# A hybrid gMLP and dilated-attention trunk on one core: side work moved between the quarters, v scaled on POOL, output combinations loaded an item ahead

## The chip, the core and the metric

The kernel runs on one core of one Trainium2 chip. The metric is the time of one execution on the device in microseconds. Three runs of the kernel before gave 2929.86, 2934.66 and 2934.5 us, median 2934.5. The engines are named as the profile names them: PE (TensorE matmul), PEld (its weight loads), DVE (VectorE), ACT (ScalarE), POOL (GpSimd), SP (SyncE, which issues the DMAs).

## The reference

The input x has 2048 rows of 1024, c is one conditioning vector. Layer A is a gated MLP whose gate mixes rows within chunks of 128; layer B is dilated sliding-window attention with 24 heads in three groups (distances 1, 4, 16), all reading one shared K/V. Everything is float32.

```
# layer A
shift, scale, gate = split(silu(c) @ ada_w + ada_b, 3)
h = rms_norm(x, norm_g) * (1 + scale) + shift
u, v, z = split(h @ w_in, 3)                   # each 2048 wide
u = gelu(u);  v = rms_norm(gelu(v), sgu_g)
mixed = einsum('gts,bcsge->bctge', tril(w_s), v per chunk) + b_s
x = x + gate * ((u * mixed * silu(z)) @ w_out)
# shared k, v from the new x: 6 heads each, k normalised
# layer B
q, z = h' @ w_in_b                             # 24 query heads, gate z
per group: softmax over the previous and own band of 128 keys, ALiBi bias, log-sum-exp
o = sum over groups of softmax(lse) * o_group
x = x + gate * ((o * silu(z)) @ w_out_b)
```

## The kernel before

The 2048 rows are worked in four quarters of 512 (Q = 0 to 3). A matrix product in float32 is done by splitting each operand into a high and a low part of the form that TensorE multiplies fast; three matmuls stand for one. Operand and weight are split by an ACT copy (L262) and a DVE subtraction (L263), 128 x 512 at a time. Large products are also done in Strassen's way: seven products of combined blocks stand for eight, with combined weights (t1 to t4) that are made once, kept in DRAM (wt, cw, wtd) and loaded again.

The order of the stages in the program is: layer A of quarter 0 (its v, u, z and its output product, L1325), layer B of quarter 0 (proj_B, L1539: blocks kv2, kv1, q2, kv0, q1, q0, z); then layer_half (L1402), which makes v, u and z of layer A for quarters 1 and 2 together: first the column blocks vh4 and vh5 of v, then eight gate blocks, each of a u part (uh0 to uh7) and a z part (zh0 to zh7); then output product and layer B of quarter 1, the same of quarter 2, layer A of quarter 3 (v3, u3, z3, output product), layer B of quarter 3, and the last attention with the final product.

Beside the products runs side work. It is written as generators in a list called fillers (L76); at certain matmuls tick (L92) adds the current rate[0] to a counter and lets the generators at the front of the list make as many steps as the counter has whole units. drain (L98) runs the list out. So a rate sets how densely a piece of side work lies beside the products, and the place in the program where it is appended sets where it begins. A scheduler then orders the instructions of each engine, and buffers come from pools with a fixed number of tiles.

The pieces of side work that the change touches are these. combine_out (L431) makes the combined output weights: for each of 8 items it loads two 512 KB tiles co (L441), subtracts among the four parts (L460), splits the results into cs and stores them with DMAs wtd<-cs (L457); an item has six steps, three of them empty ones between its loads and its first subtraction. presplit_b (L417) loads the sixteen blocks of the last output weights (pre, L411), splits them and stores the parts (wod, L407). ada_gate and ada_acc (L180, L233) make a conditioning vector on DVE from eight 512 KB loads. make_h(1) (L865) makes the second part of the normalised long input for quarters 1 and 2, with a load xa, PE transposes (pt_a, L896) and DVE scalings (h_a, L898). attend_local and near (L1836, L1839) are attention over blocks of 128 queries; there POOL makes dg (L1772), a select (L1773), an addition (L1775) and adds into pT (L1799), which PE reads (po, L1824). In the gate blocks each tile vc of v is loaded (L1440) and scaled by the rows' factor rvh on ACT (L1444) before PE mixes it (pmh, L1452). All DMAs named here are issued by SP in one order.

Of the kernel before, what the change touches and what calls it, by code (L numbers as in the profile page):

```python
# [1 line left out]

# [32 lines left out]
def trunk(ctx, tc, out, x, c, a_ada_w, a_ada_b, a_norm_g, a_w_in, a_sgu_g, a_w_spatial,  # L35
# [144 lines left out]
    def ada_acc(res, w, c0, nm):  # L180

        acc = evt(f"acc_{nm}")
        for k in range(KT):
            if k % 2 == 0:
                wt = xp.tile([P, 2, 512], F32, tag="xin", name=f"aw_{nm}{k}")
                nc.sync.dma_start(wt, w[k * P:(k + 2) * P, c0:c0 + 512].rearrange("(k p) n -> p k n", p=P))
# [46 lines left out]
    def ada_gate(w, b, i, nm):  # L233
        for h in range(2):
            res = []
            cs = slice(h * 512, (h + 1) * 512)
            yield from ada_acc(res, w, 2 * D + h * 512, f"{nm}{h}")
# [179 lines left out]
    def presplit_b():  # L417

        t = one.tile([P, 8, 512], F32R, tag="big", name="pre")
        todo = [(b_w_out[k * P:(k + 1) * P, n * 512:(n + 1) * 512], wod[n, k]) for n in range(2) for k in range(KT)]  # L420
        return presplit(todo, lambda i, u: t[:, 4 + 2 * (i % 2):6 + 2 * (i % 2), :] if u else
                        t[:, i % 4, :].bitcast(F32))

    def presplit_a():

        todo = [(a_w_out[(8 * h + 4 * r + k) * P:(8 * h + 4 * r + k + 1) * P, c * 512:(c + 1) * 512], wtd[h, 4 + r + c, k])
                for h in range(2) for r, c in ((0, 0), (1, 0), (1, 1)) for k in range(4)]
        return presplit(todo, lambda i, u: wp.tile([P, 2, 512], F32R, tag="w", name=f"was{i}") if u else
                        rp.tile([P, 512], F32, tag="raw", name=f"rawa{i}"))
# [3 lines left out]
    def combine_out():  # L433


        for h in range(2):
            for k in range(4):
                q = []
                for r in range(2):
                    t = cb.tile([P, 2, 512], F32, tag="xin", name=f"co{h}{k}{r}")  # L440
                    nc.sync.dma_start(t, a_w_out[(8 * h + 4 * r + k) * P:(8 * h + 4 * r + k + 1) * P, :]  # L441
                                      .rearrange("p (c n) -> p c n", c=2))
                    q += [t[:, c, :] for c in range(2)]
                yield
                yield
                yield
                t1, t3, t4, t2 = q
# [799 lines left out]
    def layer_A(Q, hA, m, sqv, j0):  # L1247
        if Q:
# [3 lines left out]
            rate[0] = 3.9  # L1252
# [139 lines left out]
    def in_long():  # L1392
        p = presplit_a()
        for n, _ in enumerate(attend_local(0, True)):
            if n % 4 == 3:
                next(p, None)
            if n == 50:
                rate[0] = 1.1
# [3 lines left out]
    def layer_half(ops, got):  # L1402
# [26 lines left out]
        for g in range(8):  # L1429
            if g == 2:  # L1430
# [5 lines left out]
                rate[0] = 1.7  # L1436
            vch = []
            for half in range(2):
# [100 lines left out]
    def proj_B(Q, hk, hb, keep, rest, ahead, ready):  # L1539
# [72 lines left out]
        if Q == 1:  # L1612
            rate[0] = 2.4
# [505 lines left out]
```

## Time and profile before

| what | us |
|---|---|
| runs | 2929.86, 2934.66, 2934.5; median 2934.5 |
| profiled execution | 2929.71 |
| its span, first to last instruction | 2928.0 |
| PE busy | 2858.4 (98%) |
| DVE busy | 2196.6 (75%) |
| ACT busy | 1655.4 (57%) |
| POOL busy | 756.7 (26%) |
| mean granted TensorE clock | 0.995 |

The profile is of one execution, and its times are microseconds from the start of the span. A row of a window gives the busy time of each engine in that stretch with the number of its instructions, then the granted clock of TensorE (1.00 is 2.4 GHz, 0.50 is 1.2 GHz), the mean busy share of the DMA engines, and the data rate. A row of a wait names the waiting instruction's line and the instruction or DMA that released it. In a timeline the bracket at a row's end is the idle time before it and what ended it. The stages lie, roughly, at 0 to 412 (layer A of quarter 0), 412 to 632 (layer B of quarter 0), 640 to 809 (vh4 and vh5), 810 to 1222 (gate blocks), 1222 to 1530 (quarter 1), 1530 to 1855 (quarter 2), 1855 to 2640 (quarter 3), and the rest.

### The profile page before, as it was taken

How to read it: one execution, taken by the hardware profiler on the slowest of the kernel's cores; microseconds unless marked ns; L12 is line 12 of the kernel's file. 1: busy time of each engine (PE TensorE's matmuls, PEld its weight loads, DVE VectorE, ACT ScalarE, POOL GpSimd, SP SyncE). 2: the span in 40 equal slices, each digit the busy share in tenths (PEclk: the TensorE clock that was granted, in tenths of full speed). 3: DMA queues.
4: the chain of work that ended last, by engine and by line, in shares of the span. 5: the costliest groups of instructions: out<-in, count | busy, mean ns of one | idle time of the engine just before them, and what ended most of it. 6: DMA issues, size and time to landing. Idle time of an engine off the chain costs nothing.

```text
span 2928.0 us, 45185 instructions
## 1 busy us (share of the span) xinstructions
PE 2858.4 (98%) x14450; PEld 2390.7 (82%) x14450; DVE 2196.6 (75%) x4104; ACT 1655.4 (57%) x3390; POOL 756.7 (26%) x1021
## 2 busy tenths in 40 slices
PE   8999999999999999999999999999999999999999
PEld 5788878877888787777888888888888888888887
DVE  6877468687597788867787867789779776888782
ACT  4324436666566676536564557667655366876441
POOL 1066332340000013001424224205335221222312
PEclk9999999999999999999999999999999999999999
DMA  9899786788776644687999858864337967789653
GB/s 320 288 333 342 260 287 201 231 285 287 274 266 191 212 152 165 232 316 258 315 325 329 281 175 264 292 195 138 116 110 255 334 202 227 254 269 335 221 173 110
DMA packets 388209, 718.74 MB, mean 245 GB/s; under 512 B 42010, under 2 KB 121084, under 8 KB 387588
## 3 DMA queue, kind: packets, MB, share of 16 engines
q1 hardware_dynamic: 387972, 715.87, 72.9%
q8 instruction: 114, 1.87, 0.3%
q14 instruction: 123, 1.01, 0.1%
HBM read 541.52 MB, written 174.20 MB: 244 GB/s over the span
## 4 chain that ended last, share of the span: by engine, by line
PE 71%; DVE 9%; DMA 8%; ACT 5%; issue 4%; POOL 2%; SPq 1%; POOLq 0%; DVEq 0%; ACTq 0%
PE pd_kv L291 8%; PE po L1824 3%; PE pd_o L291 2%; PE pd_u L333 2%; PE pd_u L335 2%; PE pd_u L334 2%; PE pd_z L333 2%; PE pd_z L335 2%; PE pd_z L334 2%; PE pd_v L291 2%; PE pd_o3a L291 2%; PE pq L1714 1%; PE pd_o1a L291 1%; PE pd_o2a L291 1%; PE ps L1745 1%
## 5 line engine op out<-in xcount | busy, mean ns | idle before, releaser
L291 PE MATMUL pd_kv<-w_kv,hkh 128*128 128x512 f32 x672 | 208.9, 391 | 2.3 <-DVE w_kv L263 2.0
L1824 PEld LDWEIGHTS po<-kv,pT 128*128 128x128 f32 x1200 | 149.8, 193 | 23.5 <-POOL pT L1799 9.1
L1824 PE MATMUL po<-kv,pT 128*128 128x128 f32 x1200 | 154.5, 278 | 12.8 <-POOL pT L1799 7.0
L291 PEld LDWEIGHTS pd_kv<-w_kv,hkh 128*128 128x128 f32 x672 | 125.6, 188 | 30.0 <-DVE w_kv L263 2.9
L1772 POOL TENSOR_TENSOR dg<-pr,ident 128x256 f32<-128x256 f32 x38 | 32.5, 855 | 429.6 <-ACT pr L1764 405.1
L291 PE MATMUL pd_kv<-w_kv,hkl 128*128 128x512 f32 x336 | 130.7, 389 | 0.0
L1764 ACT ACTIVATE pr<-pr,stat,rt 128x256 f32<-128x256 f32 (+1 forms) x192 | 104.2, 544 | 28.9 <-DVE stat L1761 14.2
L262 ACT ACTIVATE w_q<-raw_q 128x512 fp32r<-128x512 f32 x144 | 88.9, 627 | 54.1 <-DMA raw_q<-in_b_w_in_dram 12.2
L1588 POOL TENSOR_SCALAR s_q<-s_q 128x4 f32<-128x4 f32 x96 | 29.0, 302 | 346.6 <-DVE s_q L1587 260.7
L263 DVE TENSOR_TENSOR w_q<-raw_q,w_q 128x512 fp32r<-128x512 f32 x144 | 96.7, 693 | 26.2 <-ACT w_q L262 24.2
L2012 PE MATMUL pf<-wo,yb 128*128 128x512 f32 x256 | 104.8, 409 | 0.2 <-ACT yb L1975 0.2
L333 PE MATMUL pd_u<-hAh,w_u 128*128 128x512 f32 x256 | 103.6, 405 | 0.0
L333 PE MATMUL pd_z<-hAh,w_z 128*128 128x512 f32 x256 | 102.6, 401 | 0.0
L2014 PE MATMUL pf<-wo,yb 128*128 128x512 f32 x256 | 100.4, 392 | 0.0
L335 PE MATMUL pd_u<-hAh,w_u 128*128 128x512 f32 x256 | 100.2, 391 | 0.0
L2013 PE MATMUL pf<-wo,yb 128*128 128x512 f32 x256 | 100.2, 391 | 0.0
L335 PE MATMUL pd_z<-hAh,w_z 128*128 128x512 f32 x256 | 100.1, 391 | 0.0
L334 PE MATMUL pd_z<-hAl,w_z 128*128 128x512 f32 x256 | 99.9, 390 | 0.0
L334 PE MATMUL pd_u<-hAl,w_u 128*128 128x512 f32 x256 | 99.9, 390 | 0.0
L1764 ACT ACTIVATE st_pr<-st_pr,stat,rt 128x256 f32<-128x256 f32 (+1 forms) x128 | 73.4, 575 | 25.4 <-DVE stat L1758 14.7
L262 ACT ACTIVATE w_u<-raw_u 128x512 fp32r<-128x512 f32 x64 | 40.0, 628 | 81.4 <-PE pd_u L335 52.6
L1799 POOL TENSOR_TENSOR pT<-pT,dg 128x256 f32<-128x256 f32 x76 | 62.8, 831 | 89.1 <-DVE pT L1798 78.3
(1474 smaller groups left out, 8960.0 us busy)
## 6 DMA issues: line engine op xcount, KB each, us to landing
raw_q<-in_b_w_in_dram SPq DMA_DIRECT2D x144, 256.0 KB, 3.9
qt<-qd SPq DMA_DIRECT2D x96, 260.0 KB, 3.4
od<-ot SPq DMA_DIRECT2D x96, 256.0 KB, 3.0
w_o<-wtd SPq DMA_DIRECT2D x48, 512.0 KB, 5.6
raw_kv<-in_w_kv_dram SPq DMA_DIRECT2D x84, 256.0 KB, 3.6
kv<-kvd SPq DMA_DIRECT2D x75, 256.0 KB, 4.2
raw_u<-in_a_w_in_dram SPq DMA_DIRECT2D x64, 256.0 KB, 3.6
wt<-st_cw SPq DMA_DIRECT2D x64, 256.0 KB, 5.5
```

The costliest lines, as they stand in the source:

```text
L262: nc.scalar.activation(hi, src, AF.Copy)
L263: nc.vector.tensor_tensor(lo, src, hi.bitcast(F32), ALU.subtract)
L291: last_mm[0] = nc.tensor.matmul(pt, a, u[:, w, :], start=f, stop=e, skip_group_check=more)
L333: nc.tensor.matmul(pts[i], wh, hh[:, k, :], start=k == 0, stop=False)
L334: nc.tensor.matmul(pts[i], wh, hl[:, k, :], start=False, stop=False)
L335: nc.tensor.matmul(pts[i], wl, hh[:, k, :], start=False, stop=k == KT - 1)
L1764: nc.scalar.activation(pr[:, i, :], pr[:, i, :], AF.Exp, bias=mneg[:, i:i + 1], scale=u["rt"][:, h:h + 1], accum_out=lsum[:, i:i + 1])
L1799: nc.gpsimd.tensor_tensor(pT[:, :, 0, :], pT[:, :, 0, :], u["dg"][:, c * hp:(c + 1) * hp, :], ALU.add)
L1824: nc.tensor.matmul(po[:, h * P:(h + 1) * P], u["pT"][h // hp][:, h % hp, j, :], u["kv"][:, j, kh, 1, :], start=j == 0, stop=j == nk - 1)
L2012: nc.tensor.matmul(pt, yb[:, 0, k, :], w_[:, 0, :], start=k == 0, stop=False)
L2013: nc.tensor.matmul(pt, yb[:, 0, k, :], w_[:, 1, :], start=False, stop=False)
L2014: nc.tensor.matmul(pt, yb[:, 1, k, :], w_[:, 0, :], start=False, stop=k == KT - 1)
```

## The change

- ada_acc can be given slots: then the four 512 KB loads of a half go out at once, into a tile of their own (gbw), and the steps follow. ada_gate moves from layer B of quarter 0 to layer B of quarter 1 in this form.
- presplit_b takes its tiles from the common pools (wp, rp) and moves from layer B of quarter 1 to quarter 3, where earlier() makes one of its steps after every sixth of the attention's steps.
- make_h(1) moves from the output product of quarter 0 to layer B of quarter 0.
- combine_out loads item i + 1 when it begins item i, and has no empty steps between (two at its start remain).
- the scaling of vc goes from ACT to POOL.
- attend_local(1) beside the output product of quarter 2 does blocks 4 to 6; block 7 and the exchange of its statistics (joint) go to quarter 3.
- rates: 3.9 to 4.9 after v of quarter 3, 4.0 to 2.9 at the output product of quarter 0, 1.1 to 1.15 and 1.7 to 1.5 in the gate blocks, 3.1 to 2.6 at the output product of quarter 2, 0.7 to 0.5 in layer B of quarter 1; 2.0 for make_h(1), 1.2 for ada_gate.

```diff
@@ ada_acc
-    def ada_acc(res, w, c0, nm):
+    def ada_acc(res, w, c0, nm, slots=None):
...
+        if slots is not None:
+            for k in range(0, KT, 2):
+                load(k)
+            yield
@@ presplit_b
-        return presplit(todo, lambda i, u: t[:, 4 + 2 * (i % 2):6 + 2 * (i % 2), :] if u else
-                        t[:, i % 4, :].bitcast(F32))
+        return presplit(todo, own_tiles("b"))
+
+    def own_tiles(nm):
+        return lambda i, u: (wp.tile([P, 2, 512], F32R, tag="w", name=f"w{nm}s{i}") if u else
+                             rp.tile([P, 512], F32, tag="raw", name=f"raw{nm}{i}"))
@@ combine_out
+        nxt = load(0)
+        yield
+        yield
         for h in range(2):
             for k in range(4):
...
-                yield
-                yield
-                yield
-                t1, t3, t4, t2 = q
+                t1, t3, t4, t2 = nxt
+                if 4 * h + k < 7:
+                    nxt = load(4 * h + k + 1)
@@ layer_A
-            rate[0] = 3.9
+            rate[0] = 4.9
...
-            fillers.extend((combine_weights((4, 5), "sums"), make_h(1, affa, None)))
-            rate[0] = 4.0
+            fillers.append(combine_weights((4, 5), "sums"))
+            rate[0] = 2.9
@@ layer_half
-                    nc.scalar.activation(v[:, c, :], v[:, c, :], AF.Copy, scale=rvh[:, i:i + 1])
+                    nc.gpsimd.tensor_scalar(v[:, c, :], v[:, c, :], rvh[:, i:i + 1], None, ALU.mult)
@@ proj_B
-        if Q == 1:
-            rate[0] = 2.4
-            fillers.append(presplit_b())
...
         if Q == 0:
+            rate[0] = 2.0
+            fillers.append(make_h(1, affa, None))
+        if Q == 1:
             rate[0] = 1.2
-            fillers.append(delayed(ada_gate(b_ada_w[0], b_ada_b, 1, "gb")))
-        if Q == 1:
-            rate[0] = 0.8
+            slots = one.tile([P, 4, 2, 512], F32, tag="big", name="gbw")
+            fillers.append(delayed(ada_gate(b_ada_w[0], b_ada_b, 1, "gb", slots)))
@@ attend_local
-        bs = range(4 * Q, 4 * Q + 4)
+        bs = range(4 * Q, 4 * Q + (4 if both else 3))
@@ earlier
-        yield from near(1, True)
-        yield from attend_local(2, True)
+        p = presplit_b()
+        for n, _ in enumerate(chain(attend([(1, 7)], True, 0, 2, True), joint(1), near(1, True), attend_local(2, True))):
+            if n % 6 == 5:
+                next(p, None)
+            yield
+        yield from p
@@ main loop
-                rate[0] = 3.1
+                rate[0] = 2.6
...
-                rate[0] = 0.7
+                rate[0] = 0.5
```

How the scheduled order changes is shown at three places. The first is SP's queue at the end of the output product of quarter 0: x1d<-xr is the store that VectorE waits for, wt<-st_cw are stores of combined weights, raw_kv loads of the next weights, xa the load of make_h(1). Before:

```order
384 L381 DMA wt_0_130<-st_cw_3579 128x512
385 L381 DMA wt_1_131<-st_cw_3584 128x512
386 L381 DMA wt_2_132<-st_cw_3580 128x512
387 L381 DMA wt_3_133<-st_cw_3583 128x512
388 L270 DMA raw_kv_0_0_3774<-in_w_kv_dram 128x512
389 L270 DMA raw_kv_0_1_3779<-in_w_kv_dram 128x512
390 L270 DMA raw_kv_0_2_3784<-in_w_kv_dram 128x512
391 L270 DMA raw_kv_0_3_3789<-in_w_kv_dram 128x512
392 L270 DMA raw_kv_0_4_3794<-in_w_kv_dram 128x512
393 L270 DMA raw_kv_0_5_3799<-in_w_kv_dram 128x512
394 L871 DMA xa_4861<-in_x_dram 128x1024
395 L1344 DMA x1d<-xr_0_2853 128x1024
```

And after, at the same place:

```order
376 L391 DMA wt_2_132<-st_cw_3378 128x512
377 L280 DMA raw_o_1_7_3473<-in_a_w_out_dram 128x512
378 L391 DMA wt_3_133<-st_cw_3381 128x512
379 L280 DMA raw_kv_0_0_3672<-in_w_kv_dram 128x512
380 L280 DMA raw_kv_0_1_3677<-in_w_kv_dram 128x512
381 L280 DMA raw_kv_0_2_3682<-in_w_kv_dram 128x512
382 L280 DMA raw_kv_0_3_3687<-in_w_kv_dram 128x512
383 L280 DMA raw_kv_0_4_3692<-in_w_kv_dram 128x512
384 L280 DMA raw_kv_0_5_3697<-in_w_kv_dram 128x512
385 L1360 DMA x1d<-xr_0_2853 128x1024
```

The load xa is gone from the row ahead of the store, and the last stores wt stand among weight loads where a block of eight stood.

The second place is SP's queue in vh5, ahead of the weights of its last product (raw_vh5t from wt_3; those from wt_2 belong to the product before it). Before:

```order
705 L270 DMA raw_vh5t_1_7285<-wt_2_132 128x512
706 L270 DMA raw_vh5t_2_7290<-wt_2_132 128x512
707 L270 DMA raw_vh5t_3_7295<-wt_2_132 128x512
708 L270 DMA raw_vh5t_0_7374<-wt_3_133 128x512
709 L441 DMA co_7538<-in_a_w_out_dram 128x1024
710 L270 DMA raw_vh5t_1_7379<-wt_3_133 128x512
711 L457 DMA wtd<-cs_7225 128x1024
712 L457 DMA wtd<-cs_7228 128x1024
713 L457 DMA wtd<-cs_7259 128x1024
714 L457 DMA wtd<-cs_7262 128x1024
715 L270 DMA raw_vh5t_2_7384<-wt_3_133 128x512
716 L270 DMA raw_vh5t_3_7389<-wt_3_133 128x512
```

And after, the twelve rows up to the first load of wt_3 (the last load of wt_2 is row 708, and rows 709 to 712 are four stores wtd<-cs):

```order
713 L451 DMA co_7275<-in_a_w_out_dram 128x1024
714 L1406 DMA vh<-vh5b_7245 128x512
715 L1406 DMA vh<-vh5b_7249 128x512
716 L1406 DMA vh<-vh5b_7287 128x512
717 L1406 DMA vh<-vh5b_7291 128x512
718 L473 DMA wtd<-cs_7331 128x1024
719 L473 DMA wtd<-cs_7334 128x1024
720 L473 DMA wtd<-cs_7365 128x1024
721 L473 DMA wtd<-cs_7368 128x1024
722 L451 DMA co_7391<-in_a_w_out_dram 128x1024
723 L451 DMA co_7393<-in_a_w_out_dram 128x1024
724 L280 DMA raw_vh5t_0_7408<-wt_3_133 128x512
```

Fifteen other DMAs stand now between the loads of the two products, where the loads followed each other.

The third is POOL in the last gate blocks, where the near attention runs beside them: dg, select and addition of one head pair, then pT. Before there is nothing between them:

```order
284 L1799 TENSOR_TENSOR pT_1_10_10289<-pT_1_10_10289,dg_1_1_9988 128x2x128
285 L1799 TENSOR_TENSOR pT_1_11_10293<-pT_1_11_10293,dg_1_1_9988 128x2x128
286 L1772 TENSOR_TENSOR dg_2_1_10331<-st_pr_2_10_10317,ident 128x256
287 L1773 AFFINE_SELECT st_pr_2_10_10317<-st_pr_2_10_10317 128x2x128
288 L1775 TENSOR_TENSOR st_pr_2_10_10317<-st_pr_2_10_10317 128x2x128
```

And after:

```order
288 L1813 TENSOR_TENSOR pT_1_00_10145<-pT_1_00_10145,dg_1_0_9858 128x2x128
289 L1813 TENSOR_TENSOR pT_1_01_10149<-pT_1_01_10149,dg_1_0_9858 128x2x128
290 L1460 TENSOR_SCALAR vc_10258<-vc_10258,rvh 128x256 x4
291 L1460 TENSOR_SCALAR vc_10264<-vc_10264,rvh 128x256 x4
292 L1786 TENSOR_TENSOR dg_2_0_10187<-pr_2_00_10173,ident 128x256
293 L1787 AFFINE_SELECT pr_2_00_10173<-pr_2_00_10173 128x2x128
294 L1789 TENSOR_TENSOR pr_2_00_10173<-pr_2_00_10173 128x2x128
```

The eight scalings of a gate block stand between pT of one head pair and dg of the next.

## Rows read from the trace of the kernel before

**Rows 1.** The page, part 1: busy time of each engine, share, instructions.
```profile
PE 2858.4 (98%) x14450; PEld 2390.7 (82%) x14450; DVE 2196.6 (75%) x4104; ACT 1655.4 (57%) x3390; POOL 756.7 (26%) x1021
```

**Rows 2.** Waits of PE: waiting line, releaser, us in total, times, longest.
```profile
PE po L1824 <- POOL pT L1799: 7.0, 5, 3.9
PE pt_a L896 <- DVE h_a L898: 5.4, 5, 2.3
...
PE po L1824 <- ACT pT L1670: 4.7, 3, 2.5
...
PE pt_b L962 <- DVE xr L1354: 3.6, 1, 3.6
...
PE pd_uh6y L743 <- ACT w_uh6t L262: 2.2, 1, 2.2
...
PE pd_q11a L291 <- ACT w_q L262: 1.4, 1, 1.4
```

**Rows 3.** Windows: us, busy PE PEld DVE ACT POOL (count), PEclk, DMA share, GB/s.
```profile
410.00:415.00 5.00, 1.39 (x7) 0.91 (x6) 1.32 (x3) 0.95 (x2) 0.13 (x1) 0.81 1.02 405
415.00:420.00 5.00, 5.00 (x22) 4.41 (x20) 2.82 (x7) 0.49 (x1) 0.00 (x0) 0.51 0.80 253
```

**Rows 4.** Chain of waits, end of quarter 0: start, length, what.
```profile
406.27 7.29 DMA x1d<-xr
```

**Rows 5.** Timeline of SP, end of quarter 0.
```profile
394.79 8.01 SPq L381 DMA_DIRECT2D wt<-st_cw  x8
```

**Rows 6.** The store line L1344, all stores.
```profile
DMA to landing us min/median/max: 2.8/4.1/5.4
```

**Rows 7.** Window of make_h(0) in layer B of quarter 0.
```profile
600.00:650.00 50.00, 47.16 (x219) 37.47 (x218) 44.43 (x67) 30.60 (x53) 23.64 (x31) 1.00 0.85 280
```

**Rows 8.** Timeline of ACT, layer B of quarter 1.
```profile
1354.13 0.63 ACT L262 ACTIVATE pre<-pre 128x512 fp32r<-128x512 f32 x1 [3.83 <-DMA pre<-in_b_w_out_dram]
...
1355.52 0.37 ACT L1522 ACTIVATE hs_k<-pd_kv 128x256 f32<-128x256 f32 x1
```

**Rows 9.** Windows: layer B of quarters 1 and 2, gate blocks.
```profile
1355.00:1360.00 5.00, 2.31 (x8) 1.59 (x7) 3.46 (x7) 3.10 (x7) 2.21 (x4) 0.86 0.43 160
1360.00:1365.00 5.00, 4.44 (x11) 3.00 (x10) 1.72 (x3) 1.88 (x4) 0.30 (x1) 0.50 0.70 185
1698.00:1736.00 38.00, 38.00 (x169) 31.48 (x168) 28.15 (x47) 23.99 (x42) 12.22 (x25) 1.00 0.68 204
955.00:960.00 5.00, 3.92 (x16) 3.48 (x17) 2.88 (x6) 5.00 (x12) 0.00 (x0) 0.66 0.34 106
```

**Rows 10.** Groups by line: busy us, mean ns, idle before, releasers.
```profile
L263 DVE TENSOR_TENSOR w_q<-raw_q,w_q 128x512 fp32r<-128x512 f32 x144 | 96.7, 693 | 26.2 <-ACT w_q L262 24.2 <-DMA qd<-st_q31w 0.9
...
L263 DVE TENSOR_TENSOR w_z<-raw_z,w_z 128x512 fp32r<-128x512 f32 x64 | 58.0, 919 | 31.2 <-ACT w_z L262 29.8 <-DMA st_cw<-in_b_w_in_dram 1.2
...
L1772 POOL TENSOR_TENSOR dg<-st_pr,ident 128x256 f32<-128x256 f32 x38 | 33.5, 880 | 76.8 <-ACT st_pr L1764 67.0 <-DVE stat L1758 2.9 <-DVE stat L1784 2.4
...
L1444 ACT ACTIVATE vc<-vc,rvh 128x256 f32<-128x256 f32 x64 | 27.1, 497 | 15.9 <-DMA vc<-vh 12.7 <-POOL rvh L1427 3.2
...
L1773 POOL TENSOR_SCALAR_AFFINE_SELECT st_pr<-st_pr 128x256 f32<-128x256 f32 x38 | 19.1, 503 | 2.8
```

**Rows 11.** Timeline of ACT in the gate blocks.
```profile
953.06 2.49 ACT L1444 ACTIVATE vc<-vc,rvh 128x256 f32<-128x256 f32 x6
...
1109.75 2.49 ACT L1444 ACTIVATE vc<-vc,rvh 128x256 f32<-128x256 f32 x6
```

**Rows 12.** Windows: a stretch with full queues, and product vh5.
```profile
200.00:250.00 50.00, 50.00 (x247) 42.29 (x246) 31.35 (x33) 16.89 (x27) 33.72 (x25) 1.00 1.02 346
733.00:809.00 76.00, 76.00 (x337) 62.91 (x336) 44.27 (x70) 43.35 (x89) 0.00 (x0) 1.00 0.81 279
```

**Rows 13.** Tile raw_vh5t, its loads.
```profile
DMA to landing us min/median/max: 2.8/3.3/3.8
```

**Rows 14.** Window in the u product of quarter 3.
```profile
1983.70:2003.40 19.70, 19.70 (x127) 17.44 (x126) 19.66 (x52) 12.82 (x30) 13.00 (x16) 1.00 0.43 133
```

More of the change, by code (lines that the diff above doesn't have):

```diff
@@ L1 @@
 from contextlib import ExitStack
+from itertools import chain
 import numpy as np
@@ L177, in trunk, with load @@
                             channel_multiplier=-1)
-    def ada_acc(res, w, c0, nm):
+    def ada_acc(res, w, c0, nm, slots=None):
         acc = evt(f"acc_{nm}")
+        def load(k):
+            wt = xp.tile([P, 2, 512], F32, tag="xin", name=f"aw_{nm}{k}") if slots is None else slots[:, k // 2]
+            nc.sync.dma_start(wt, w[k * P:(k + 2) * P, c0:c0 + 512].rearrange("(k p) n -> p k n", p=P))
+            return wt
+        if slots is not None:
+            for k in range(0, KT, 2):
+                load(k)
+            yield
         for k in range(KT):
             if k % 2 == 0:
-                wt = xp.tile([P, 2, 512], F32, tag="xin", name=f"aw_{nm}{k}")
-                nc.sync.dma_start(wt, w[k * P:(k + 2) * P, c0:c0 + 512].rearrange("(k p) n -> p k n", p=P))
+                wt = load(k) if slots is None else slots[:, k // 2]
             if k == 0:
@@ L231, in ada_affine, with ada_gate @@
         later.append([2, lambda: nc.vector.scalar_tensor_tensor(dst[0], dst[0], 1.0, go, ALU.add, ALU.mult)])
-    def ada_gate(w, b, i, nm):
+    def ada_gate(w, b, i, nm, slots=None):
         for h in range(2):
@@ L427, in presplit_a, with load @@
                 for h in range(2) for r, c in ((0, 0), (1, 0), (1, 1)) for k in range(4)]
-        return presplit(todo, lambda i, u: wp.tile([P, 2, 512], F32R, tag="w", name=f"was{i}") if u else
-                        rp.tile([P, 512], F32, tag="raw", name=f"rawa{i}"))
+        return presplit(todo, own_tiles("a"))
     made = [False]
     def combine_out():
+        def load(i):
+            h, k = divmod(i, 4)
+            q = []
+            for r in range(2):
+                t = cb.tile([P, 2, 512], F32, tag="xin", name=f"co{h}{k}{r}")
+                nc.sync.dma_start(t, a_w_out[(8 * h + 4 * r + k) * P:(8 * h + 4 * r + k + 1) * P, :]
+                                  .rearrange("p (c n) -> p c n", c=2))
+                q += [t[:, c, :] for c in range(2)]
+            return q
+        nxt = load(0)
+        yield
+        yield
         for h in range(2):
             for k in range(4):
[L438 to L443, printed above, removed]
-                yield
-                yield
-                yield
-                t1, t3, t4, t2 = q
+                t1, t3, t4, t2 = nxt
+                if 4 * h + k < 7:
+                    nxt = load(4 * h + k + 1)
                 def keep(*todo):
@@ L1397, in in_long @@
             if n == 50:
-                rate[0] = 1.1
+                rate[0] = 1.15
             yield
@@ L1435, in layer_half @@
                 fillers.append(in_long())
-                rate[0] = 1.7
+                rate[0] = 1.5
             vch = []
@@ L1632, in proj_B @@
         if Q < NQ - 1:
[L1633 to L1634 removed]
+            drain()
             ahead()
@@ L1839, in attend_local, with joint @@
     def attend_local(Q, wrap=False, alt=False, both=True):
-        bs = range(4 * Q, 4 * Q + 4)
+        bs = range(4 * Q, 4 * Q + (4 if both else 3))
         yield from attend([(1, b) for b in bs], wrap, int(alt), 1 + (wrap or alt), wrap or alt)
+        if both:
+            yield from joint(Q)
+            yield from near(Q, wrap, alt)
+    def joint(Q):
         v = stat[1][:, 4 * Q:4 * Q + 4, :]
@@ L1846, in attend_local @@
         nc.sync.dma_start(v, std[1].rearrange("(b i) c -> i b c", i=P)[:, 4 * Q:4 * Q + 4])
-        if both:
-            yield from near(Q, wrap, alt)
     outs = []
```

5 lines of the change are left out of this document (1 added, 4 removed).

## Prediction

> **What bounds the kernel now.** I read the busy line of the page first, then what PE waited for, then short windows round the longest of these waits, and there the timeline of the engine named. PE is busy for 98% of the span [rows 1], and both versions give it the same 13,342 matmuls, so the change can act only on what PE loses: 2928.0 - 2858.4 = 69.6 us of idle time, and the stretches in which its clock is granted at half. The idle time lies in many small places; the longest stand in [rows 2]. A stall can cost twice: at the end of quarter 0 PE does 1.39 us of work in five microseconds, and then works five microseconds at a granted clock of 0.51 [rows 3]. The full-speed work in those ten is 1.39 + 5.00 x 0.51 = 3.9 us, so the place costs 6.1 and not the 3.6 that the waits name. I size every term in this way: idle time, and behind it the busy time at half clock.
>
> **End of quarter 0: -5.5.** PE's first normalisation transposes of layer B (pt_b) wait for VectorE's xr, and that waits for the stores x1d<-xr: 7.29 us from the first one's issue until VectorE can go on [rows 4]. Ahead of it SP has issued eight stores of combined weights in 8 us [rows 5] and, right before it, the load xa of make_h(1); the DMA share is 1.02 while the store is out [rows 3]. In the changed order no load for make_h stands there: six raw_kv loads and then the store, and of the eight stores of combined weights four lie further ahead and four are spread among weight loads. The 16 stores of the line land in 2.8 to 5.4 us, 4.1 in the middle [rows 6]; with 4.1 for the 7.29 the stall of 3.6 shrinks to 0.4. What could remain is the whole term if the kv loads alone fill the queues: -6.1 with 0 as its other end; I take -5.5.
>
> **make_h(1) moved from the output product to layer B of quarter 0: -2.3, +2.** PE waits 2.3 us for h_a once [rows 2], in the product that make_h(1) leaves. It comes back in q02/kv00, where the conditioning (16 accumulations on VectorE) leaves. The nearest row for the same work inside layer B is make_h(0) in the stretch 600 to 650, with 2.84 us idle [rows 7]. I take +2 (0 to +5).
>
> **Layer B of quarter 1: -7.** The weight presplit leaves. There ScalarE sits 3.83 us until a presplit load has landed, and the evacuation hs_k of the PSUM tile that the next product needs stands behind it [rows 8]. The ten microseconds from 1355 hold 2.31 x 0.86 + 4.44 x 0.50 = 4.2 us of full-speed work [rows 9], so 5.8 are lost; a second place of the same kind costs the 1.4 of pd_q11a [rows 2]. Together -7.2. At the same product of quarter 2, without presplit, PE never stops: 38.00 of 38.00 [rows 9]. What comes in instead is ada_gate: eight 512 KB loads, in two groups of four issued at once, and sixteen 128x512 VectorE operations; its 11 us of VectorE (16 x 0.69, the mean of w_q in [rows 10]) I cost at nothing, hidden by VectorE's idle time, which is 9.85 of 38 us at this place of quarter 2 [rows 9]; if that cover is gone, I would give PE at most 3 of the 11. I take -7 (-8 to -3).
>
> **Gate blocks: -6.** The scaling of v goes from ScalarE to POOL: 64 instructions of 497 ns [rows 10]. Two PE stalls hang on them. At 953.06 six scalings (2.49 us) stand ahead of the pT copy for which PE waits 2.5 [rows 2, 11], followed by a clock of 0.66 on 3.92 busy microseconds (1.3 lost) [rows 9]. At 1109.75 another six push the exponentials and three table loads back until w_uh6t comes 2.2 late [rows 2, 11], with about 0.7 at half clock. 2.5 + 1.3 + 2.2 + 0.7 = 6.7. On POOL one 128x256 instruction takes between 0.50 (a select) and 0.88 us (two inputs) [rows 10]; a scaling has one input and no predicate, so I take 0.55. In six of the eight blocks POOL has nothing else to do. In the last two its queue holds the scalings in front of dg and pT of the near attention, where PE already waits for POOL 3.9 us once [rows 2]: eight scalings of 0.55 are 4.4 us in that queue, of which 0 to 4 reach PE; I take +1. The first block's eight scalings end about 1 us later (8 x 0.55 against 3.31), +0.5. Net -5 (-11 to +5).
> VectorE's 128x512 subtraction takes 919 ns on average where POOL combines weights beside it, and 693 in the query weights of layer B [rows 10]. The Trainium skill (GPSIMD Engine Reference, section 1, Specifications) says that POOL shares its SBUF interfaces with VectorE, and that VectorE instructions with two SBUF inputs suffer; the two rows agree. By that rule 64 x 0.55 = 35 us of POOL work would lengthen what VectorE does beside them by up to a third, an estimate of 9 us in the stage; by the rows' bare durations it would be nothing. That is the second rival.
>
> **Output combinations loaded an item ahead: +8.** This is what I fear most. combine_out waits for nothing at each item now, so it takes three turns in place of six, and its transfers fall together in the product of vh5: by the order 4 more loads and 10 more stores, 14 x 0.52 = 7.3 MB, less 1.2 of loads that move on to the gate blocks. The stretch 733 to 809 carries 279 GB/s x 76 us = 21.2 MB [rows 12]; with 6.1 more it asks for 359 GB/s. In fifty microseconds with all queues full the core moved 346 [rows 12]. On SP the four weight loads of the last product (raw_vh5t from wt_3) stood among the loads before; now eight stores wtd<-cs, three co loads and four vh stores stand between the loads from wt_2 and them: 4.2 + 1.6 + 1.0 = 6.8 MB, 20 us at 346 GB/s, and 3 us for the four loads themselves. Between the first use of one product's weights and of the next lie 48 matmuls of 76.00/337 = 0.2255 us [rows 12], 10.8 us, and the wt_2 loads are themselves issued about one product ahead. So 23 us stand against 22, and then come the landing's end (a set's loads land in 3.3 us when nothing is ahead of them [rows 13]), a copy of 0.63 on ScalarE and 0.69 on VectorE: 2 to 5 us too late, and a piece at half clock as at 415 (5.00 x 0.49 = 2.5) [rows 3]: 4.5 to 7.5, and something at the product before, whose lead shrinks as well. I take +8 (0 to +16), since nothing in the trace excludes that SP runs ahead of this order.
> The Trainium skill (DMA: Bandwidth & Descriptors, Where 436 GB/s comes from) gives 358 GB/s as the limit between HBM and one core, and lets it bind. That is 359 against 358, a tie: an estimate of no stall by bandwidth; by the trace's 346 the stage is 3 us short. One stretch of five microseconds shows 405 [rows 3], so the figure is no wall here, and I stay with the 346 of the long stretch.
> What goes is VectorE's wait for the co loads (each lands in about 5 us), but vh5, where most of these waits lie, costs PE nothing before (76.00 of 76.00 busy [rows 12]), and in vh4 the first items stand in the order where they stood, so 0.
>
> **Quarter 2: -2.** Block (1,7) of the attention and its statistics leave layer_out: three blocks for four. Of the 7.0 us that PE waits for POOL's pT, 3.1 lie in four waits under 3.9 [rows 2], most of them there; I take -2 (-4 to 0).
> **Quarter 3: +3.** The block, the presplit (16 loads, 16 ScalarE copies, 16 VectorE subtractions, 16 stores) and a faster rate of side work (4.9 for 3.9) come into u and z. VectorE gets 16 x 0.69 = 11 us and a block's share. It is already full in one stretch, 19.66 of 19.70, where PE still does not stop [rows 14]; the DMA share there is 0.43. So neither stops PE as it is, and what is added lies within about 270 us. Bounds 0 and +8 (most of the 11 us, where they fall on a full VectorE). The other rates that change (1.1 to 1.15, 1.7 to 1.5, 0.7 to 0.5, 3.1 to 2.6, 4.0 to 2.9) place the same side work a little earlier or later among the products; I cost them at nothing, between -2 and +2.
>
> **Sum.** -5.5 - 2.3 + 2 - 7 - 5 + 8 - 2 + 3 = -8.8, about -9 on the profiled execution's 2929.7 (span 2928.0 and 1.7 round it): 2921. The three runs shown are 2929.9, 2934.5 and 2934.7, so the profiled one is at their lower end, and the same -9 from the median gives 2925.5. I take 2922, nearer to the sum since the changed kernel's runs may fall at either end. 0.2% is 5.9 us and about what this kernel's measurement can tell from no change: faster is below 2928.6, slower above 2940.4.
>
> **Rivals.**
> 1. The weights of vh5 starve PE throughout (slower). For it: 359 GB/s asked where 346 were seen; each late set costs 3.3 (landing) [rows 13] + 0.63 [rows 8] + 0.69 = 4.6 us and then about 2.5 at half clock. It decides if SP is held at the stores, so that five sets come late and not one: 5 x 7 = 35 in place of 8, 2949. Three late sets give 21 and 2935. Against it: before, the weights stand well ahead, and stores wait only for copies that VectorE, with 44.27 of 76 busy [rows 12], does early.
> 2. POOL is the wrong place for the scalings (no change): dg and pT come 4 us later in two blocks, VectorE is up to 9 us slower beside POOL, and the -5 turns to +5: 2932. For it: PE already waits 3.9 for POOL, and 919 against 693; against it: POOL is empty in six blocks.
> 3. Quarter 3 can't take the presplit (no change): VectorE full for the added 11 us, +8 and half clock behind it, 2930.
> 4. The change does not do what it says: the kv loads alone make the store late, and the gate's 2 MB at once delay the weights of quarter 1; -5.5 and -7 become -2 and -3: 2930.
>
> **How the numbers follow.** Forecast 0.60 with its own range 2912 to 2930; rival 1 0.16 (two thirds of it slower), rival 2 0.11, rival 3 0.07, rival 4 0.06. Faster: 0.60 x 0.93, and a third of the rest of the mild cases, 0.63. Slower: 0.11 from rival 1, and 0.05 from two of the others together, 0.16. The rest, 0.21, is no change. Range 2907 to 2941: the lower end takes the better ends of vh5 (0) and of the gate blocks, the upper one stops between the two prices of rival 1.
>
> **What would show it.** At the end of quarter 0: x1d under 5 us, and no clock of 0.51 behind it. Layer B of quarter 1: no wait of pd_q12b for hs_k. Gate blocks: no vc on ScalarE, PE's waits for pT of ScalarE and for w_uh6t gone; rival 2 if PE's wait for POOL's pT grows over 7.0. In vh5: PE waiting for w_vh5t or its loads shortly before the first gate block, with a DMA share near 1; without such a wait the +8 is wrong and the time is near 2914. Quarter 3: PE waits in u and z between block 7's operations. If PE's idle time falls by less than 4 us in all, the forecast is wrong.

## The result, and the profile after

The changed kernel takes 2941.8 us (median of 15 runs, 2933.3 to 2949.8) beside 2934.5 for the kernel before (15 runs, 2929.2 to 2942.6): ratio 1.0024, 95% interval 1.0013 to 1.0034. It is a little slower. I had forecast 2922 and a range up to 2941. The profiled executions are 2939.5 (span 2937.8) and 2929.7 (span 2928.0), 9.8 us apart, and the traces account for that.

The first lines of the page after, which answer to [rows 1]: the same 14,450 PE instructions, and idle time of 2937.8 - 2863.8 = 74.0 us, where it was 69.6.

```profile
span 2937.8 us, 45193 instructions
## 1 busy us (share of the span) xinstructions
PE 2863.8 (97%) x14450; PEld 2392.8 (81%) x14450; DVE 2216.8 (75%) x4104; ACT 1639.8 (56%) x3335; POOL 815.2 (28%) x1085
```

What PE waited for, after (waiting line, releaser, us in total, times, longest), against [rows 2]: of the longest waits before, that for xr falls from 3.6 to 0.5. The wait for POOL's pT doubles, in many short pieces where there was one of 3.9, and two new waits of 4.8 and 4.7 stand below it.

```profile
PE po L1838 <- POOL pT L1813: 14.2, 13, 1.7
...
PE pmh L1468 <- POOL vc L1460: 4.8, 1, 4.8
PE pd_vh5a L301 <- ACT w_vh5t L272: 4.7, 1, 4.7
...
PE po L1838 <- ACT pT L1684: 3.6, 4, 1.3
...
PE pt_b L978 <- DVE xr L1370: 0.5, 1, 0.5
```

To place the time by stage I take PE's lost time: from each matmul's start to the next one's, less the median of that distance for matmuls of the same shape before, summed over the stage. It holds idle time, half clock, and the small gaps of a mixed stream. It sums to 117.6 us before and 127.0 after, 9.4 more, nearly the 9.8 by which the executions differ. In quarters 1 to 3 the row of the output product ends at the first q block of layer B, so it holds the two kv blocks before that as well.

| stage | before | after | forecast | measured |
|---|---|---|---|---|
| quarter 0 up to the output product | 26.2 | 24.3 | 0 | -1.9 |
| output product of quarter 0 | 9.8 | 0.1 | -7.8 | -9.7 |
| layer B of quarter 0 | 5.0 | 4.8 | +2 | -0.1 |
| vh4 | 4.4 | 4.2 | 0 | -0.3 |
| vh5 | -0.1 | 8.5 | +8 | +8.6 |
| first gate block, uh0 and zh0 | 0.5 | 7.2 | +0.5 | +6.7 |
| the other gate blocks | 23.9 | 14.9 | -5.5 | -9.0 |
| output product, quarter 1 | 5.7 | 5.6 | 0 | -0.1 |
| layer B of quarter 1 | 7.9 | 0.4 | -7 | -7.5 |
| output product, quarter 2 | 7.4 | 8.2 | -2 | +0.8 |
| layer B of quarter 2 | 0.2 | 0.2 | 0 | 0 |
| v, u, z of quarter 3 | 4.3 | 25.6 | +3 | +21.3 |
| the rest | 22.6 | 23.1 | 0 | +0.5 |

Two windows of after show the places that were mended, the end of quarter 0 (against [rows 3]; start:end, length, busy PE PEld DVE ACT POOL with counts, PEclk, DMA share, GB/s) and the start of q12 in quarter 1 (against the first two of [rows 9]): PE never stops and the clock stays at 1.00. In the first, the store x1d is issued at 396.78 and VectorE's xr follows at 399.84 without a wait.

```profile
395.00:400.00 5.00, 5.00 (x23) 4.13 (x22) 4.05 (x9) 2.79 (x7) 1.46 (x3) 1.00 0.50 195
400.00:405.00 5.00, 5.00 (x31) 4.16 (x30) 4.11 (x8) 1.49 (x3) 0.94 (x1) 1.00 0.72 225
```
```profile
1343.20:1405.60 62.40, 62.40 (x270) 49.50 (x270) 48.67 (x81) 30.12 (x54) 29.21 (x40) 1.00 0.76 242
```

vh5 after (the second row of [rows 12] answers): the queues carry 329 GB/s at a share of 0.93, and after PE's stop the clock is 0.50 for five microseconds. The chain of waits names the load: raw_vh5t, issued at 784.39, takes 5.80 where such loads took 2.8 to 3.8 [rows 13], and the copy and PE follow it. With the 3.3 that was the middle there it would have come 2.5 us earlier; so, as an estimate, half of PE's 4.7 is the load's longer way and the other half its late issue, behind the fifteen other DMAs.

```profile
733.00:790.00 57.00, 52.77 (x232) 43.01 (x230) 38.68 (x63) 31.23 (x66) 0.00 (x0) 1.00 0.93 329
790.00:795.00 5.00, 3.77 (x9) 2.93 (x10) 4.93 (x9) 4.36 (x8) 0.00 (x0) 0.50 1.01 373
```
```profile
784.39 5.80 DMA raw_vh5t<-wt
...
790.55 0.64 ACT w_vh5t L272
...
791.24 1.22 PE pd_vh5a L301 x2
```

The first gate block after. The tile vc (instruction, count, shortest, median and longest in ns): a scaling takes 0.92 us on POOL in the middle, against 0.50 on ACT [rows 10]. In POOL's timeline the eight of the first block end at 818.6, and they start only at 811.29, behind the row factors rvh: on VectorE the sum uh0t stands ahead of these and waits for its load raw_uh, issued at 802.52 and 4.99 us under way.

```profile
L1460 POOL TENSOR_SCALAR vc<-vc,rvh x64: 917/922/1742, 811.3 to 1166.6; 128x256 f32<-128x256 f32 x64
```
```profile
808.46 0.57 POOL L1442 TENSOR_SCALAR rvh<-rvh 128x8 f32<-128x8 f32 x1 [176.13 <-DVE rvh L1441]
809.12 2.07 POOL L1443 TENSOR_TENSOR rvh<-rvh,mhalf 128x8 f32<-128x8 f32 x1
811.29 7.31 POOL L1460 TENSOR_SCALAR vc<-vc,rvh 128x256 f32<-128x256 f32 x8
```

The row factors are late only for a changed order. VectorE has their sums 3.5 us after the block's first matmul (808.21 and 804.71); before it was 5.4 (815.30 and 809.91), and PE did not wait. But the first mixing matmul pmh stood behind 48 of the block's matmuls before and stands behind 12 now. On PE, before and after:

```profile
820.79 1.05 PE L1452 MATMUL pmh<-wst,vc 128*128 128x128 f32 x8
```
```profile
804.71 2.88 PE L759 MATMUL pd_uh0x<-op,w_uh 128*128 128x512 f32 x12
812.35 0.79 PE L1468 MATMUL pmh<-wst,vc 128*128 128x128 f32 x2 [4.76 <-POOL vc L1460]
```

Quarter 3, where most is lost. v, u and z as one window, before and after: PE's idle time goes from 352.10 - 351.04 = 1.1 to 390.70 - 375.06 = 15.6 us, while no engine is full (VectorE 320 of 391, POOL 135). Eleven waits for pT make 12.2 of it (the waits of PE in this stretch); the time at half clock behind them is lost as well.

```profile
1876.20:2228.30 352.10, 351.04 (x1962) 302.03 (x1960) 282.23 (x609) 230.10 (x462) 113.01 (x160) 1.00 0.49 156
```
```profile
1855.30:2246.00 390.70, 375.06 (x2114) 322.41 (x2112) 320.14 (x690) 261.15 (x519) 135.13 (x190) 0.99 0.56 181
```

```profile
PE po L1838 <- POOL pT L1813: 12.2, 11, 1.7
```

One of these waits, on POOL and on PE. PE has transposed pp of one step of the attention at 2163.16, and VectorE's part of pT is done at 2166.4. But the two additions into pT that are left stand in POOL's queue among the work of the next step (dg, a select and an addition, twice over), which waits for that step's exponential (ACT, 2163 to 2165). The last ends at 2171.5, and PE comes to po twice before its half is done.

```profile
2164.52 0.74 POOL L1786 TENSOR_TENSOR dg<-st_pr,ident 128x256 f32<-128x256 f32 x1 [3.38 <-ACT st_pr L1778]
2165.34 0.41 POOL L1787 TENSOR_SCALAR_AFFINE_SELECT st_pr<-st_pr 128x256 f32<-128x256 f32 x1
2165.83 0.74 POOL L1789 TENSOR_TENSOR st_pr<-st_pr 128x256 f32<-128x256 f32 x1
2166.52 1.19 POOL L1786 TENSOR_TENSOR dg<-st_pr,ident 128x256 f32<-128x256 f32 x1
2167.68 1.17 POOL L1813 TENSOR_TENSOR pT<-pT,dg 128x256 f32<-128x256 f32 x1
2168.81 0.86 POOL L1787 TENSOR_SCALAR_AFFINE_SELECT st_pr<-st_pr 128x256 f32<-128x256 f32 x1
2169.75 1.04 POOL L1789 TENSOR_TENSOR st_pr<-st_pr 128x256 f32<-128x256 f32 x1
2170.75 0.72 POOL L1813 TENSOR_TENSOR pT<-pT,dg 128x256 f32<-128x256 f32 x1
```
```profile
2163.16 0.60 PE L1806 MATMUL pp<-ident,pr 128*128 128x128 f32 x4
2168.90 1.16 PE L1838 MATMUL po<-kv,pT 128*128 128x128 f32 x8 [1.02 <-POOL pT L1813]
2171.53 1.63 PE L1838 MATMUL po<-kv,pT 128*128 128x128 f32 x8 [1.47 <-POOL pT L1813]
```

From the last pp transposes to the first po PE took 6.15 us in the middle before (18 cases) and 5.32 after (22 cases), its stops included. From the same transposes to the end of the second addition into pT POOL's queue took 4.8 in the middle before and 5.7 after: what fitted does not fit any more.

### The profile page after: what moved, and what is told of

The parts are those of the page before. It is cut to its first block, busy times and chain, and to the rows that moved or that the text cites. A ratio compares the mean times of both kernels' runs of the same rounds, so it can differ in the third digit from the quotient of the medians.

```text
span 2937.8 us, 45193 instructions
## 1 busy us (share of the span) xinstructions
PE 2863.8 (97%) x14450; PEld 2392.8 (81%) x14450; DVE 2216.8 (75%) x4104; ACT 1639.8 (56%) x3335; POOL 815.2 (28%) x1085
## 4 chain that ended last, share of the span: by engine, by line
PE 73%; DVE 9%; DMA 7%; issue 4%; ACT 3%; POOL 2%; SPq 1%; POOLq 0%; DVEq 0%; ACTq 0%
PE pd_kv L301 7%; PE po L1838 3%; PE pd_o L301 3%; PE pd_v L301 2%; PE pd_z L345 2%; PE pd_z L344 2%; PE pd_z L343 2%; PE pd_o3a L301 1%; PE pd_u L345 1%; PE pd_u L343 1%; PE pd_u L344 1%; PE pd_v3a L301 1%; PE pd_vh4a L301 1%; PE pd_o1a L301 1%; PE pd_v3b L301 1%
## 5 line engine op out<-in xcount | busy, mean ns | idle before, releaser
L1460 POOL TENSOR_SCALAR vc<-vc,rvh 128x256 f32<-128x256 f32 x64 | 61.3, 975 | 190.1 <-DMA vc<-vh 138.2
```

## The experiments

Each undoes a part of the change in the changed kernel. Beside a time stands that of the kernel before on the same chip. All but the last two are single runs, and eleven runs of the kernel before in one series spread from 2920.6 to 2937.3; so a few us between two times say little, and the argument goes by lost times by stage, as above, from one profiled execution each. In runs whose edit leaves a stage alone, vh5 loses 6.0 to 8.5, the first gate block 6.8 to 9.2, uh1 to uh7 12.6 to 15.1, and v, u and z of quarter 3 25 to 30.

**combine_out as before.**

```diff
...
-        nxt = load(0)
-        yield
-        yield
...
-                t1, t3, t4, t2 = nxt
-                if 4 * h + k < 7:
-                    nxt = load(4 * h + k + 1)
+                yield
+                yield
+                yield
+                t1, t3, t4, t2 = q
```

> The changed kernel, with combine_out as before (loads at the head of an item, three empty steps). In the changed kernel PE loses 8.5 us in vh5 (a wait of 4.7 for w_vh5t, and half clock) and 7.2 in the first gate block (a wait of 4.8 for vc). Theory A: both come from the dense transfers; the weights raw_vh5t arrive late, and the load raw_uh that VectorE waits for ahead of the row factors rvh arrives late too. Then vh5 falls to about 0 and the first gate block to 2 or 3: 12 us less, 2929. Rival B: the wait for vc is the price of the scalings on POOL and the place of the first mixing matmul on PE, and has nothing to do with the loads. Then vh5 falls to 0 and the first gate block stays near 7: 8 us less.

2932.5 beside 2928.2. vh5 loses nothing again (-0.1), so the dense transfers were the whole of its 8.5. The first gate block keeps 7.0: for that, rival B seemed right. The first mixing matmul is back behind 48 others, so this edit undoes the order too. PE comes to it later, but the eight scalings took 10.94, and PE still waits 3.1 for vc:

```profile
804.61 10.94 POOL L1455 TENSOR_SCALAR vc<-vc,rvh 128x256 f32<-128x256 f32 x8
```

**Scalings of v on ScalarE.**

```diff
-                    nc.gpsimd.tensor_scalar(v[:, c, :], v[:, c, :], rvh[:, i:i + 1], None, ALU.mult)
+                    nc.scalar.activation(v[:, c, :], v[:, c, :], AF.Copy, scale=rvh[:, i:i + 1])
```

> The changed kernel, with the 64 scalings of v on ScalarE as before. Theory A (late loads hold up rvh): in the first gate block PE still waits, for ScalarE's vc now, some 3 of the 7.2 us; rival B (POOL's price): the first block falls under 1. In the other gate blocks (uh1 to uh7: 23.8 us lost before, 14.9 after) both expect the loss to come back to 20 to 24, with PE's waits for the pT copy of ScalarE and for w_uh6t, so that the whole is within 5 us of the changed kernel.

2936.9 beside 2928.2. The first gate block loses 6.5 all the same: now PE waits 1.4 for w_uh0t and 2.0 for ScalarE's vc, behind the load raw_uh of which VectorE's row tells.

```profile
806.79 0.69 DVE L741 TENSOR_TENSOR uh0t<-raw_uh,uh0t 128x512 f32<-128x512 f32 x1 [1.98 <-DMA raw_uh<-in_w_uz_dram]
807.40 0.16 DVE L1441 TENSOR_REDUCE rvh<-sqh 128x4 f32<-128x16 f32 x1
```

Both theories had missed in part, and what both expected of the other blocks was wrong: they lose 15.7, not 20 to 24. The waits for pT do not come back. That for ScalarE's w_uh6t does, 2.2 before and 1.2 after (with 0.8 more for VectorE's half):

```profile
PE pd_uh6y L759 <- ACT w_uh6t L272: 2.3, 1, 2.3
```

**combine_out as before, and the first block's scalings on ScalarE.**

```diff
...
-                    nc.gpsimd.tensor_scalar(v[:, c, :], v[:, c, :], rvh[:, i:i + 1], None, ALU.mult)
+                    if g == 0:
+                        nc.scalar.activation(v[:, c, :], v[:, c, :], AF.Copy, scale=rvh[:, i:i + 1])
+                    else:
+                        nc.gpsimd.tensor_scalar(v[:, c, :], v[:, c, :], rvh[:, i:i + 1], None, ALU.mult)
```

> The changed kernel with combine_out as before, and with the eight scalings of the first gate block on ScalarE (the other 56 on POOL). Each edit alone left the first gate block at 6.5 to 7 us lost: without the dense loads PE waited for POOL's scalings (three places of 0.4 and one of 3.3), with the scalings on ScalarE it waited for the late row factors. Theory E: the block has two causes, and each covers the other. Then with both undone it falls under 2, and with vh5 at 0 the whole is some 14 us under the changed kernel, 2925. Rival F: the cause is a third one, the place of the mixing matmuls in the order; then it stays above 4.

2929.1 beside 2929.0 (the median of the eleven runs of before in that series). vh5 -0.1, first block 0.1: theory E. The dense transfers and the slow scalings each fill the same gap, and only without both it closes. Rival F is not settled by it: the first mixing matmul is behind 48 others here too, so late loads and changed order went together, and no run parts them.

**Block (1,7) back in quarter 2, rates 3.1 and 3.9.**

```diff
...
-            rate[0] = 4.9
+            rate[0] = 3.9
...
-        bs = range(4 * Q, 4 * Q + (4 if both else 3))
+        bs = range(4 * Q, 4 * Q + 4)
...
-                rate[0] = 2.6
+                rate[0] = 3.1
```

> The changed kernel, with attention block (1,7) back beside the output product of quarter 2, and the rates of before there (3.1) and in quarter 3 (3.9); the presplit stays in quarter 3. From v of quarter 3 to its output product PE loses 4.3 us before and 25.6 after, most of it in eleven waits of 1.2 to 1.9 for POOL's pT. Theory C: the higher rate and the added block put the attention's steps so close together on PE that the chain of exponentials, three POOL instructions and the two pT additions isn't done when PE comes to po. Then the loss falls to 5 to 8: 18 us less. Rival D: the presplit's copies and subtractions stand in that chain on ScalarE and VectorE. Then the loss stays above 15.

2919.3 beside 2928.2. v, u and z of quarter 3 lose 6.1, and 0.9 is left of the waits for pT, with the presplit still among them:

```profile
PE po L1838 <- POOL pT L1813: 0.9, 1, 0.9
```

**The presplit behind the attention.**

```diff
-            if n % 6 == 5:
-                next(p, None)
             yield
         yield from p
```

> The changed kernel, with the presplit's steps behind the attention of quarter 3 and not between its steps; block (1,7) and the rate 4.9 stay. Rival D (the presplit stands in the attention's chain): the loss from v to the output product of quarter 3 falls from 25.6 to under 10, and 15 us are gained. Theory C (rate and block): it stays above 18, and the time changes by less than 6 us.

2964.3 beside 2928.2. u and z still lose 22.0, so the presplit is not the cause; rival D falls. Behind them something new came up: the output product of quarter 3 loses 37.5 (3.4 before), with 17.1 us of waits for its weights w_o3t, which SP issues among the presplit's loads and stores. Behind the attention the presplit costs more than between its steps.

**Rate 3.9 alone.**

```diff
-            rate[0] = 4.9
+            rate[0] = 3.9
```

> The changed kernel with the rate 3.9 of before in u and z of quarter 3; block (1,7) and the presplit stay there. With block and rate both undone the loss from v to the output product of quarter 3 fell from 25.6 to 6.1. Theory C1 (the rate alone sets how close the attention's steps lie): the loss in u and z falls under 8, and what does not fit comes behind, in the output product, where it may cost. Theory C2 (the added block takes its toll by its own instructions): it stays above 15.

2945.3 beside 2929.0. u and z lose 9.2; the block is there, and the waits are gone (1.1 us for pT in all). What does not fit runs behind, and the row of the output product loses 28.6. Theory C1.

**Rate 4.9 alone, the block in quarter 2 with its rate 3.1.**

```diff
-        bs = range(4 * Q, 4 * Q + (4 if both else 3))
+        bs = range(4 * Q, 4 * Q + 4)
...
-                rate[0] = 2.6
+                rate[0] = 3.1
```

> The changed kernel with block (1,7) back beside the output product of quarter 2, but the rate 4.9 kept in u and z of quarter 3. With block and rate undone the loss there was 6.1, with the rate alone undone 9.2, and 28.6 came behind it in the output product. Theory C1 (the rate spaces the steps): with 4.9 the waits for POOL's pT are back, 15 to 25 us. Theory C2 (the block): they are gone, under 9.

2934.2 beside 2932.3. 22.5 lost, without the block, and the waits are back:

```profile
PE po L1838 <- POOL pT L1813: 11.1, 10, 3.3
```

With the run before it this settles quarter 3. The higher rate costs 16.4 with the block (25.6 against 9.2) and 16.4 without it (22.5 against 6.1); the block costs 3.1 at either rate, and at 3.9 it does not fit. In the middle of the cases the way to the second addition into pT takes 5.3 and 5.5 in the two runs at 3.9, where PE takes 6.2 from transposes to po, and 5.8 here, where PE takes 5.7.

**The gate blocks' rates of before.**

```diff
-                rate[0] = 1.15
+                rate[0] = 1.1
...
-                rate[0] = 1.5
+                rate[0] = 1.7
```

> The changed kernel with the gate blocks' rates of before (1.7 and 1.1 for 1.5 and 1.15). The blocks uh1 to uh7 lose 23.8 us before and 14.9 after; with the scalings back on ScalarE they still lose 15.7, so the scalings are not what helped. Theory G: the lower rate is, since the attention's steps lie further apart. Then the loss comes back to 20 or more, about +8 us. Rival H: something else is (the combinations of the output weights are done earlier, and their stores and splits no longer lie in these blocks). Then it stays under 17.

2938.3 beside 2929.0. The blocks uh1 to uh7 lose 15.7: by the sum rival H as against G. But the waits are others. The longest of before is back:

```profile
PE po L1838 <- POOL pT L1813: 3.9, 1, 3.9
```

The three runs with the rates of before (this one, the kernel before and the next) have 3.6 to 3.9 there, and none of the other eleven has it. The eleven, the changed kernel among them, wait 2.2 to 3.5 for w_uh7t, and the three do not; in the changed kernel:

```profile
PE pd_uh7y L759 <- ACT w_uh7t L272: 2.3, 1, 2.3
```

So the rate decides both waits, and they nearly cancel in the sum.

**combine_out, scalings and gate rates as before, all three** (the diffs of those runs together).

> The changed kernel with all edits to the gate stage undone together: combine_out as before, all scalings on ScalarE, rates 1.7 and 1.1. Each alone left the blocks uh1 to uh7 at 15 to 16 us lost, against 23.8 before. Theory I (any one of the edits is enough, they cover one another): with all undone the loss is back at 22 to 25. Theory J (the two long waits of before are an accident of how loads fall, which any shift of the stage ends): it stays at 13 to 18.

2932.9 beside 2932.3. Now the loss is back at 22.3, with the waits of [rows 2] in their old size (the gate blocks alone):

```profile
PE po L1833 <- POOL pT L1808: 3.6, 1, 3.6
PE po L1833 <- ACT pT L1679: 2.7, 2, 2.5
PE pd_uh6y L754 <- ACT w_uh6t L272: 2.2, 1, 2.2
```

So no edit has the 9 us by itself. The wait for POOL's pT goes with the rates. That for ScalarE's pT is in the kernel before and here, and neither with the rates of before alone nor with the scalings on ScalarE alone; whether combine_out matters for it was not tried. That for w_uh6t never goes.

**make_h(1) back in the output product of quarter 0.**

```diff
-            fillers.append(combine_weights((4, 5), "sums"))
-            rate[0] = 2.9
+            fillers.extend((combine_weights((4, 5), "sums"), make_h(1, affa, None)))
+            rate[0] = 4.0
```

> The changed kernel with make_h(1) back in the output product of quarter 0, at the rate 4.0, and out of layer B of quarter 0. The product loses 9.8 us before and 0.1 after. If the prediction's step holds (its load stands ahead of the store x1d, and its scalings wait on VectorE), the loss is back at 7 to 10, with a wait of PE for xr. A rival: the conditioning's move out of layer B of quarter 0 emptied the queues; then the loss stays under 4.

2955.4 beside 2932.3. The product loses 11.4 again, and both its waits return (PE's waits in this product and the kv blocks behind it). On SP the load xa and the stores wt stand ahead of x1d once more. The rate came back with the move, so the two are not parted; 5 us more are lost in other stages.

```profile
PE pt_b L978 <- DVE xr L1370: 4.0, 1, 4.0
PE pt_a L912 <- DVE h_a L914: 2.3, 2, 2.0
```

**Three parts undone: combine_out, the first block's scalings, block (1,7) with its rates** (again the diffs above together).

> The changed kernel with three things undone: combine_out as before, the first gate block's scalings on ScalarE, block (1,7) back in quarter 2 with the rates 3.1 and 3.9. If the causes found add up, vh5 gives 8.5, the first gate block 5 to 7, and quarter 3 with quarter 2 together 20: about 33 us under the changed kernel, 2907 beside 2934.5 of before, a ratio of 0.990. If the edits cover one another as in the first gate block, half of it: 2920.

2905.8 (6 runs, 2898.5 to 2909.0) beside 2929.0: ratio 0.9920, interval 0.9895 to 0.9944. It beats both kernels (the changed one has 1.0024). vh5 loses -0.1, the first gate block 1.6, u and z of quarter 3 6.0; 94.0 us are lost in all, 33 less than in the changed kernel.

**The same with all scalings on ScalarE.**

> The version with combine_out as before and block (1,7) in quarter 2, with all 64 scalings on ScalarE in place of 8 on ScalarE and 56 on POOL (2905.8 beside 2929.0 of before, ratio 0.992). If POOL is worth anything there, this is 3 us or more slower in the blocks uh1 to uh7; if not, the two agree within 3 us, since the changed kernel with the scalings on ScalarE lost 15.7 there and 14.9 with them on POOL. I expect agreement.

2909.3 (4 runs) beside 2932.3: ratio 0.9932, interval 0.9915 to 0.9950. The intervals overlap, so the times show no worth of the move of v's scaling to POOL. The stage speaks for a small one, against what I expected: uh1 to uh7 lose 18.5 here and 14.6 in the run before, 3.9 more, with 2.6 for 1.3 in the wait for w_uh6t, in one execution each.

## Why the prediction was wrong

**The step that failed** is quarter 3: "neither stops PE as it is, and what is added lies within about 270 us", +3 with +8 as its end, where +21.3 came. I asked whether an engine is full, by [rows 14], and none is. What counts there is the distance of one step of the attention from the next, and the rate that sets it was named beside the presplit but had no term of its own. 4.9 for 3.9 puts a fifth less matmul time between a step and the next, and POOL's queue up to pT, which fits in the 6.15 us of before, does not fit any more. The runs with block and rate changed apart show it: the rate has 16.4, the block 3.1, and the presplit at most 1.8 (4.3 before, 6.1 with the presplit alone there). Rival 3 named the place with the wrong cause (VectorE full) and less than half of the price.

**The second failure** is the first gate block, +0.5 where +6.7 came. Two terms were too small. The scaling on POOL was 0.55 in the sum and measured 0.92, past the upper bound of 0.88 that I had taken from a two-input instruction. And I did not follow the denser combine_out past vh5: raw_uh landed late, VectorE stood at its sum, and the row factors behind it came too late for an order in which PE asks for them 36 matmuls sooner. I had it as the cause of one stall, and it made two, the second hidden behind POOL's. Whether loads or order weigh more there stays open.

**Right, in mechanism and size:** the output product of quarter 0 (-7.8 forecast, -9.7 measured, and back with make_h(1) and its rate), layer B of quarter 1 (-7, -7.5), and vh5 (+8, +8.6), where the wait, the load behind it and the half clock came as written. In layer B of quarter 1 the waits named are gone (3.3 for hs_k, 1.4 at pd_q11a), but no run puts the presplit back, and the change also drains the side work there, which its list leaves out; so this cause is argued and not shown. vh5 was the danger that I feared most, and it was in the sum.

**Right in sign, in part wrong in cause:** the other gate blocks, -5.5 and -9.0. I gave the gain to the scalings' move and put the rates at nothing. Of the two stalls named, that behind ScalarE's pT is gone, but that for w_uh6t is not (2.2, and 1.2 + 0.8 after). The wait for POOL's pT, to which I had added 1, lost its 3.9, and that is the rates' work. With the scalings alone back on ScalarE the gain stays. Rival 2 (POOL as the wrong place) holds for the first block alone.

Its other half, VectorE slower beside POOL, is not the scalings' work; it goes mostly with the rates. In these blocks VectorE's subtractions of the output weights take 683 ns before and 757 after; with the scalings on ScalarE they take 760, and with the scalings on POOL at the rates of before 692. In this order:

```profile
L263 DVE TENSOR_TENSOR was<-rawa,was 128x512 fp32r<-128x512 f32 x24 | 16.4, 683 | 1.4 <-ACT was L262 1.2
L273 DVE TENSOR_TENSOR was<-rawa,was 128x512 fp32r<-128x512 f32 x24 | 18.2, 757 | 0.6 <-ACT was L272 0.6
L273 DVE TENSOR_TENSOR was<-rawa,was 128x512 fp32r<-128x512 f32 x24 | 18.3, 760 | 0.6 <-ACT was L272 0.6
L273 DVE TENSOR_TENSOR was<-rawa,was 128x512 fp32r<-128x512 f32 x24 | 16.6, 692 | 3.0 <-ACT was L272 2.8
```

The rule of the Trainium skill (GPSIMD Engine Reference, section 1, Specifications), that VectorE instructions with two SBUF inputs suffer beside POOL, gave rival 2 its estimate of 9 us. These rows show nothing of that from the scalings; the rule itself agrees with the subtractions beside POOL's work in quarter 3, 0.98 in place of 0.69 (last section).

**Wrong, small:** quarter 2, -2, where +0.8 came: with one block less the waits for POOL's pT there went only from 2.4 to 2.0. make_h(1) in layer B of quarter 0 cost nothing (+2 forecast). The heading -6 of the gate blocks stands beside a net of -5, which the sum uses; the 13,342 matmuls stand in no row (the trace counts 14,450 in both versions), and nothing hangs on them.

With the two failed terms at their measured size, 18.3 and 6.2 more, the forecast sum of -8.8 becomes +15.7; the other terms gave 6.3 more than forecast, which makes the 9.4.

## What to carry to other kernels

Where side work runs beside matmuls at a set rate, a higher rate is a change in latency: before raising it, measure in the trace how long the longest chain between two of its steps takes and how much matmul time lies between them, since no engine need be full for PE to stop. When transfers are packed closer, follow every load of the next stage, not only the one that is late first. Where two causes fill the same gap, undoing one shows nothing; undo both before a cause is dropped. And compare the waits of a stage, not only its sum: one wait may have gone and another come.

## What the runs showed of the hardware

- POOL's multiplication by one factor for each partition, 128x256, takes 0.92 us in the middle and up to 1.74; the eleven that VectorE's work hardly overlapped took 0.92 as well. That is longer than POOL's two-input additions of that size (0.74 and 0.72 in the timeline above). Eight took 7.31 us in one kernel and 10.94 in another.
- In the wait of quarter 3 shown above POOL and VectorE are slower side by side. While VectorE's four subtractions of 128x512 run, POOL's two-input instructions take 1.04 to 1.19 in place of 0.74, and the one behind them 0.72 again; the subtractions take 3.93 / 4 = 0.98 in place of the 0.69 of [rows 10]:

```profile
2166.28 3.93 DVE L273 TENSOR_TENSOR w_z<-raw_z,w_z 128x512 fp32r<-128x512 f32 x4
```
